# The second block of a weight sum: added by a transfer of POOL's queue, or by VectorE from a second tile

## The chip, the cores and the metric

The kernel runs on one core of a Trainium2 chip. The metric is the time of one execution in device microseconds (us). The core's engines run side by side, each in its own order: TensorE (PE, with PEld for its weight loads), VectorE (DVE), ScalarE (ACT), GpSimd (POOL) and SyncE (SP). SP, POOL and ACT also issue transfers (DMA); 16 DMA engines carry them out.

## The reference

A decoder layer in float32 on 512 tokens of width 2048. One input projection feeds two sorts of attention heads, eight MLA heads and eight forgetting-attention (FoX) heads; their gated outputs go through one output projection.

```python
h = _rms_norm(x, g_pre)
proj = h @ w_in                                   # 2048 x 6472
q_lat, kv_lat, k_rope_raw, gate_mla, fq, fk, fv, f_logit, gate_fox = split(proj)
o_mla = _mla_branch(q_lat, kv_lat, k_rope_raw, ..., w_uq, w_ukv, cos, sin) * silu(gate_mla)
o_fox = _fox_branch(fq, fk, fv, f_logit, b_forget) * silu(gate_fox)
o = concatenate([o_mla, o_fox], axis=-1) @ w_out  # 2048 x 2048
x = x + _rms_norm(o, g_post)
```

## The kernel before

**Matmuls.** Every float32 product is made of three passes: a weight is divided into a high part `whi` (ACT's copy) and a low part `wlo` (DVE's subtraction), the activations likewise, and `mm3` multiplies high by high, high by low and low by high.

**Chunks.** The weights are cut into 220 chunks, most of 128 x 1024 (512 KB), numbered in the order of their use. `load(i)` issues the transfer of chunk i into a raw place (`raw`), `divide(i)` makes `whi` and `wlo` of it, and the matmuls read these. `chunk(i)` is called when PE's code comes to chunk i: it loads up to `ahead_load` chunks ahead, divides up to `ahead` chunks ahead. A raw place is free again when its chunk has been divided. `raw_tile(i)` chooses the place: the pool `wp` (three), and beside it, by a rule on i, the pool `vr` in the first stage, `rw` (`deep`) in the middle stage, and `op` (`more`) in the last.

**Strassen-like products.** Four large projections, "v" (the FoX values), "l" (the latents), "m" (the MLA gate) and "o" (the output projection), use seven products of half-size blocks instead of eight: p1, p2, p4, q6, g5, g7, g3. Four of the seven multiply by a sum of weight blocks: p4 by t4, q6 by t6, g5 by t5, g7 by t7. t6 and t7 (for "o" also t4) are made in DRAM beside other work, in steps that `paced` counts off by `set_pace`: SP copies the first block, and a transfer of POOL's queue adds the second (`add_step`, line 320). The sums t4 and t5 of "v", "l" and "m" and t5 of "o" are used once, so they are not made in DRAM: the chunk is loaded from its first block and gets its second on the core. They are 32 chunks in eight fours:

- "v": 29 to 32 (g5) and 49 to 52 (p4)
- "l" and "m": 97 to 100 (p4 "l"), 105 to 108 (p4 "m"), 113 to 116 (g5 "m"), 121 to 124 (g5 "l")
- "o": 188 to 191 and 200 to 203 (the halves of g5)

For these, `load(i)` issues a second transfer on SP's queue into a tile `second`, and `join(i)` (line 269) adds it to the raw place on DVE, just before the division or one or two chunks ahead of it. `second` comes from `vr` (two) in "v", from `rw` (three, `EXTRA`) in "l" and "m", and otherwise from the general pool of 28 slots.

**Names in the rows.** PSUM banks name the products: `vg` is g5 and g3 of "v", `vp` p4 of "v", `gbl` p4 "l", `gbm` p4 "m", `gdl` g5 "l", `gdm` g5 and g3 of "m", `od` g5 and g3 of "o". `smg`, `sog` are activation sums divided for these products on the core; `awaymg`, `awayog` are such sums stored in DRAM by POOL and fetched again by SP (`bmg`, `bmq`, `bog`). `v_away` are stores of the FoX values, `ghf` and `gf` steps of the FoX gate, `lat` copies of the latents from PSUM. In rows of instructions the names carry their number.

**What sets the order.** The source order is spread over the engines by a scheduler that also places transfers; each engine then runs its row in order. A transfer on SP's or POOL's queue that must wait holds all that stand behind it in that row.

Of the kernel before, what the change touches and what calls it, by code (L numbers as in the profile page):

```python
# [12 lines left out]
F32 = mybir.dt.float32  # L13
# [3 lines left out]
ALU = mybir.AluOpType  # L17
AX = mybir.AxisListType

P = 128  # L20
# [24 lines left out]
KL = L4 + ROPE  # L45
HALF = S // 2
NSLOT = 28
DEEP, EXTRA = 6, 3


def split_const(c, bits, n):
# [15 lines left out]
def tile_hybrid_layer(  # L67
# [16 lines left out]
    nc = tc.nc  # L84
    pe, act, dve, pool = nc.tensor, nc.scalar, nc.vector, nc.gpsimd
# [10 lines left out]
    vr = v_room.enter_context(tc.tile_pool(name="vr", bufs=5))  # L96
# [3 lines left out]
    def slot(name, dt=F32, shape=(P, 2, S)):  # L100

        return sp.tile(list(shape), dt, tag="s", name=name)
# [105 lines left out]
    def add_chunks(w, cols, nk, per, width, first_k=0, single=0):  # L208


        first = len(chunks)
        k = 0
        while k < nk:
            n = min(1 if k < single else per, nk - k)
            chunks.append((w, cols, first_k + k, n, width))
            k += n
        return range(first, len(chunks))

    raws, ready, up_chunks, early = {}, {}, set(), set()

    more, deep, seconds = [], [], [vr, 2]
    needs = {}

    def raw_tile(i):
        if deep and deep[1] <= i < deep[2] and (i - deep[1]) % (DEEP + 3) < DEEP:
            return deep[0].tile([P, 1024], F32, tag="raw", name=f"raw{i}", bufs=DEEP)
        if i in up_chunks:
            return slot(f"raw{i}", shape=(P, 1024))
        if i <= prods["g7", "v"][-1] and i % 5 < 2:
            return vr.tile([P, 1024], F32, tag="raw", name=f"raw{i}", bufs=2)  # L230
        pool = more[0] if more and (i - more[1]) % 6 < 3 else wp
        return pool.tile([P, 1024], F32, tag="raw", name=f"raw{i}", bufs=3)

    def load(i, small=None):

        w, cols, k, n, width = chunks[i]
        assert state["step"] >= needs.get(i, -3) + 2
        if cols is None:

            raw = raw_tile(i)  # L240
            for a, b in alike(raw, w):
                nc.sync.dma_start(a, b)
            raws[i] = raw
            if k is not None:
                if seconds and i not in early:
                    pool, bufs = seconds
                    second = pool.tile([P, 2, 512], F32, tag="second", name=f"second{i}", bufs=bufs)
                else:
                    second = slot(f"second{i}")
                nc.sync.dma_start(second, k)  # L250
                raws[i] = raw, second.rearrange("p k c -> p (k c)")
            return
        if i < 2:
            raw = slot(f"raw{i}", shape=(P, 1024))
        else:
            raw = raw_tile(i)
        v = raw[:, : n * width].rearrange("p (k c) -> p k c", k=n)
        for at, off, cnt in cols:
            (nc.sync if cnt >= P or small is None else small).dma_start(
                v[:, :, at : at + cnt],  # L260
                w[0, k * P : (k + n) * P, off : off + cnt].rearrange("(k p) c -> p k c", p=P),
            )
        raws[i] = raw

    def join(i):

        if isinstance(raws.get(i), tuple):
            raw, second = raws[i]
            tc.keep_in_program_order(dve.tensor_tensor(out=raw, in0=raw, in1=second, op=ALU.add))  # L269
            raws[i] = raw  # L270

    def divide(i):
        w, cols, k, n, width = chunks[i]
        m = n * width
        join(i)
        raw = raws.pop(i)
        hi = wp.tile([P, 1024], F32R, tag="whi", name=f"whi{i}")
        lo = wp.tile([P, 1024], F32R, tag="wlo", name=f"wlo{i}")
        cast = act.copy(hi[:, :m], raw[:, :m])  # L279
        if deep:  # L280
            tc.keep_in_program_order(cast)
        dve.tensor_tensor(out=lo[:, :m], in0=raw[:, :m], in1=hi[:, :m].bitcast(F32), op=ALU.subtract)  # L282
        ready[i] = [t[:, :m].rearrange("p (k c) -> p k c", k=n) for t in (hi, lo)]

    state = {"loaded": 0, "divided": 0, "tiles": 0, "step": -1, "pace": 4}

    def prepare(i):
        while state["divided"] < min(len(chunks), i + 1):
            divide(state["divided"])
            state["divided"] += 1  # L290

    def chunk(i, ahead_load=4, ahead=2):
        upto = i + ahead_load
        if deep:
            upto = max(upto, min(i + DEEP + 2, deep[2] - 1, state["loaded"] + i % 2))
        while state["loaded"] < min(len(chunks), upto + 1):
            load(state["loaded"])
            state["loaded"] += 1
        prepare(i + ahead)
        for k in range(i + ahead + 1, min(state["loaded"], i + ahead + (3 if deep else 2))):  # L300
            join(k)
        return ready.pop(i)

    W, made = {}, {}
# [2 lines left out]
    def alike(to, w):  # L307

        if len(w.shape) == 4:
            to = to.rearrange("p (k h x) -> p k h x", k=2, h=4)  # L310
            return [(to[:, k], w[:, k]) for k in range(2)]
        return [(to if len(w.shape) == 2 else to.rearrange("p (k c) -> p k c", k=2), w)]
# [31 lines left out]
    prods = {}  # L344
# [45 lines left out]
    for n in ("g0", "p1", "g1", "p2", "g2", "s5", "q0", "s3", "k0", "s6", "p4", "s7",  # L390
              "q1", "k1", "q2", "k2", "q3", "k3", "g3"):
        name = {"p1": "p1", "p2": "p2", "p4": "p4", "s5": "g5", "s3": "g3", "s6": "q6", "s7": "g7"}.get(n)
        if name:
            add_products([(name, "v")], plain_in)
            if n == "s5":
                early.update(prods["g5", "v"][2:])
        else:
            at = {"q": O_FQ, "k": O_FK, "g": O_GF}[n[0]] + 256 * (3 - int(n[1]))
            fox[int(n[1])][n[0]] = add_chunks(w_in, [(0, at, 256)], NK, 4, 256)
# [9 lines left out]
    for n in ("q0", "p1", "k0", "q6", "p2", "p4", "g7", "q1", "g5", "k1", "g3", "q2", "k2", "q3", "k3"):  # L409
# [5 lines left out]
        p = int(n[1])  # L415
# [62 lines left out]

    load_x_tile(0)
    load(0, act)  # L480
    load_x_tile(1)
    load(1, act)
    load_x_part(1)
    load(2, act)
# [73 lines left out]
    def set_pace(n):  # L558
        state.update(pace=n, tiles=0)
# [685 lines left out]
    c22 = v_block("vc22")  # L1245
    scaled(c22, G, 2, pb, ALU.subtract, rcol)
    todo.extend([*f3, *rot[10:14], *d3, *rot[14:]])
    set_pace(8)
    q, wholes = fox_q(0)
    drain()  # L1250
    product("g3", "v", operand("g3", "m"), G, False, True)
# [3 lines left out]
    k = fox_k(0, wholes)  # L1255
# [17 lines left out]
    scaled(c21, C, 2, c21_sum, col=rneg)  # L1273
    v_out(c21, 1, 0)
    keys = [load_keys(6 + i, wholes) for i in range(2)]
    seconds.clear()
    v_room.close()
    pp = heads_room.enter_context(tc.tile_pool(name="pp", bufs=2, reuse_waits="tile"))
    set_pace(4.9)
# [3 lines left out]
    for p in range(4):  # L1283
        if p:
# [6 lines left out]
            k = fox_k(p, wholes)  # L1291
# [163 lines left out]
            state["loaded"], prods["g3", "m"][-1] + 1,  # L1455
        ]
    )
    seconds.extend([deep[0], EXTRA])
    for j in (1, 0):
        todo.append(  # L1460
            lambda j=j: todo.extendleft(
# [75 lines left out]
    for f in range(4, 8):  # L1537
        todo.append(lambda f=f: gate(f, c12, c22))
    deep.clear()
    seconds.clear()  # L1540
    room.close()
    pp = heads_room.enter_context(tc.tile_pool(name="pp", bufs=2, reuse_waits="tile"))
    qnh, qnl = zip(*(latents[i] for i in range(6)))
# [64 lines left out]
    for p in range(4):  # L1608
# [22 lines left out]
        k, kw = mla_k(p, wholes)  # L1631
# [157 lines left out]
    op = ctx.enter_context(tc.tile_pool(name="op", bufs=8, reuse_waits="tile"))  # L1789
# [10 lines left out]
    f = og_of[1, 0]  # L1800
# [30 lines left out]
    v = three(0, C, G, f)  # L1831
# [47 lines left out]
```

## Time and profile before

| what | value |
|---|---|
| runs shown (three) | 892.56, 892.96 and 895.5 us |
| median | 892.96 us |
| span of the profiled execution | 892.3 us |
| granted TensorE clock, mean | 0.998 |
| busy: PE / DVE / ACT / POOL | 880.3 / 660.2 / 462.1 / 72.8 us |
| DVE's joins (line 269) | 32, 39.0 us |
| transfers | 225.07 MB, mean 252 GB/s |

The span reaches from the first to the last instruction of the profiled execution; the page gives no other time of that execution. A group's row gives busy time, mean ns of one and the engine's idle time before it. In a row of a tile, three durations in ns (lowest, median, highest) are followed by the first and the last start in us. A row of a stretch gives busy time by engine, the granted clock, the mean busy share of the 16 DMA engines (it can read a little above 1) and the rate. The stages lie at about: "v" 64 to 230 us, FoX heads to 420, "l" and "m" 418 to 587, MLA heads to 713, "o" from there on.

### The profile page before, as it was taken

Reading aid. Unit: us, or ns where it says so; the run is one execution under the profiler, and the core shown is the slowest. Engines: PE = TensorE matmul, PEld = TensorE weight load, DVE = VectorE, ACT = ScalarE, POOL = GpSimd, SP = SyncE. Lnnn points to the kernel's source line nnn. Section 1 sums busy time; section 2 is a strip of 40 time slices with the busy share of each in tenths; the row PEclk is TensorE's granted clock in tenths of the full one; section 3 lists DMA queues with packets and bytes.
Section 4 is the critical chain, followed back from the end, with each engine's and each line's share of the span. In section 5 each row is a group of like instructions: output and inputs, shape, how many; then the busy total and the mean of one; then the engine's idle time right before and its main releaser. Section 6 shows DMA issues by size and latency. Waiting matters only on the chain.

```text
span 892.3 us, 12700 instructions
## 1 busy us (share of the span) xinstructions
PE 880.3 (99%) x4486; PEld 748.2 (84%) x4486; DVE 660.2 (74%) x1106; ACT 462.1 (52%) x841; POOL 72.8 (8%) x92
## 2 busy tenths in 40 slices
PE   9999999999999999999999999999999999999996
PEld 9988887888888888888998999788888888888885
DVE  4579995648665546477678999979787895988786
ACT  6944434334343433335455565657465776646383
POOL 0110110011110211010000000000000000000021
PEclk9999999999999999999999999999999999999999
DMA  9998798889999999997799885697988637799878
GB/s 319 277 265 241 212 341 279 250 214 315 261 282 275 238 230 225 247 231 186 243 412 410 329 303 178 167 275 166 221 182 215 153 111 233 228 323 322 264 214 254
DMA packets 139235, 225.07 MB, mean 252 GB/s; under 512 B 16898, under 2 KB 68892, under 8 KB 138148
## 3 DMA queue, kind: packets, MB, share of 16 engines
q1 hardware_dynamic: 124660, 184.19, 63.5%
q0 software_dynamic: 13776, 39.85, 22.2%
q8 instruction: 35, 0.57, 0.2%
q10 hardware_dynamic: 736, 0.22, 0.1%
q14 instruction: 28, 0.23, 0.1%
HBM read 209.53 MB, written 69.22 MB: 312 GB/s over the span
## 4 chain that ended last, share of the span: by engine, by line
PE 91%; DVE 4%; DMA 2%; ACT 2%; issue 1%; DVEq 0%; ACTq 0%; SPq 0%
PE fq L150 3%; PE fk L150 3%; PE fk L152 3%; PE fk L151 3%; PE fq L152 3%; PE fq L151 3%; PE fg L150 3%; PE in L614 3%; PE fg L151 3%; PE fg L152 3%; PE sm L657 3%; PE mq L152 2%; PE mq L150 2%; PE mq L151 2%; PE oa L150 2%; PE oa L152 2%
## 5 line engine op out<-in xcount | busy, mean ns | idle before, releaser
L282 DVE TENSOR_TENSOR wlo<-raw,whi 128x1024 fp32r<-128x1024 f32 (+3 forms) x220 | 261.0, 1189 | 134.0 <-ACT whi L279 125.8
L279 ACT CAST whi<-raw 128x1024 fp32r<-128x1024 f32 (+3 forms) x220 | 224.3, 1023 | 233.5 <-PE fk L151 31.8
L150 PE MATMUL fk<-h,whi 128*128 128x512 f32 x128 | 52.6, 411 | 0.0
L150 PE MATMUL fq<-h,whi 128*128 128x512 f32 x128 | 50.9, 397 | 0.0
L150 PE MATMUL fg<-h,whi 128*128 128x512 f32 x128 | 50.3, 393 | 0.0
L152 PE MATMUL fk<-h,wlo 128*128 128x512 f32 x128 | 50.2, 392 | 0.0
L151 PE MATMUL fk<-h,whi 128*128 128x512 f32 x128 | 50.2, 392 | 0.0
L152 PE MATMUL fq<-h,wlo 128*128 128x512 f32 x128 | 50.0, 391 | 0.0
L151 PE MATMUL fq<-h,whi 128*128 128x512 f32 x128 | 49.9, 390 | 0.0
L152 PE MATMUL fg<-h,wlo 128*128 128x512 f32 x128 | 49.9, 390 | 0.0
L151 PE MATMUL fg<-h,whi 128*128 128x512 f32 x128 | 49.9, 390 | 0.0
L675 ACT ACTIVATE pf<-pf,stf 128x128 f32<-128x128 f32 (+3 forms) x32 | 18.0, 562 | 61.4 <-DVE stf L666 61.4
L269 DVE TENSOR_TENSOR raw<-raw,second 128x1024 f32<-128x1024 f32 x32 | 39.0, 1219 | 0.5 <-DMA second<-in_w_out_dram 0.5
L614 PE MATMUL in<-whi,h 128*128 128x328 f32 x128 | 30.0, 321 | 0.0
L150 PE MATMUL mq<-ln,whi 128*128 128x512 f32 x72 | 29.2, 406 | 0.0
L152 PEld LDWEIGHTS fk<-h,wlo 128*128 128x128 f32 x128 | 24.1, 188 | 5.5
L152 PEld LDWEIGHTS fq<-h,wlo 128*128 128x128 f32 x128 | 24.0, 188 | 5.3
L152 PEld LDWEIGHTS fg<-h,wlo 128*128 128x128 f32 x128 | 24.0, 188 | 5.2
L151 PE MATMUL mq<-ln,whi 128*128 128x512 f32 x72 | 28.3, 393 | 0.0
L152 PE MATMUL mq<-ln,wlo 128*128 128x512 f32 x72 | 28.2, 392 | 0.0
L151 PEld LDWEIGHTS fg<-h,whi 128*128 128x128 f32 x128 | 24.1, 188 | 4.7
L150 PEld LDWEIGHTS fg<-h,whi 128*128 128x128 f32 x128 | 24.1, 188 | 4.7
(610 smaller groups left out, 2417.5 us busy)
## 6 DMA issues: line engine op xcount, KB each, us to landing
raw<-in_w_in_dram SPq DMA_DIRECT2D x96, 512.0 KB
raw<-in_w_out_dram SPq DMA_DIRECT2D x32, 512.0 KB
second<-in_w_in_dram SPq DMA_DIRECT2D x24, 512.0 KB
bmg<-awaymg SPq DMA_DIRECT2D x20, 256.0 KB
awaymg<-rmg POOLq DMA_DIRECT2D x8, 512.0 KB, 6.8
raw<-t6v SPq DMA_DIRECT2D x8, 512.0 KB
t7o<-in_w_out_dram SPq DMA_DIRECT2D x4, 1024.0 KB
t7o<-in_w_out_dram POOLq DMA_DIRECT2D x4, 1024.0 KB, 10.6
```

The source lines that it names most:

```text
L150: pe.matmul(o, ah, bh, start=first, stop=False, **kw)
L151: pe.matmul(o, ah, bl, start=False, stop=False, **kw)
L152: pe.matmul(o, al, bh, start=False, stop=last, **kw)
L269: tc.keep_in_program_order(dve.tensor_tensor(out=raw, in0=raw, in1=second, op=ALU.add))
L279: cast = act.copy(hi[:, :m], raw[:, :m])
L282: dve.tensor_tensor(out=lo[:, :m], in0=raw[:, :m], in1=hi[:, :m].bitcast(F32), op=ALU.subtract)
L614: pe.matmul(banks[t][:, :n], a[k][:, tss[t]], b[:, j, :], start=k == 0 and m == 0, stop=k == NK - 1 and m == 2,)
L657: pe.matmul(s[:, :nn], a[:, qs], c[:, :nn], start=(i == 0), stop=(i == len(pairs) - 1))
L675: act.activation(p, p, AF.Exp, bias=st[:, 0:1], scale=unit, accum_out=st[:, 1:2])
```

## The change

The second block goes straight into the raw place: `load` issues, on POOL's queue, a transfer that adds it there. `join`, the tiles `second` and what chose their place are gone. The room of the second tiles becomes raw places: `vr` has four instead of two (chunks by i % 7 < 4), `rw` nine instead of six (`DEEP`). `chunk` loads two further ahead in "v" and, through `DEEP`, eleven instead of eight in "l" and "m". One pace is 7 instead of 8.

```diff
-DEEP, EXTRA = 6, 3
+DEEP = 9
...
-        if i <= prods["g7", "v"][-1] and i % 5 < 2:
-            return vr.tile([P, 1024], F32, tag="raw", name=f"raw{i}", bufs=2)
+        if i <= prods["g7", "v"][-1] and i % 7 < 4:
+            return vr.tile([P, 1024], F32, tag="raw", name=f"raw{i}", bufs=4)
...
             raws[i] = raw
             if k is not None:
-                if seconds and i not in early:
-                    pool, bufs = seconds
-                    second = pool.tile([P, 2, 512], F32, tag="second", name=f"second{i}", bufs=bufs)
-                else:
-                    second = slot(f"second{i}")
-                nc.sync.dma_start(second, k)
-                raws[i] = raw, second.rearrange("p k c -> p (k c)")
+                pool.dma_start(raw.rearrange("p (k c) -> p k c", k=2), k, accum_op=ALU.add)
             return
...
-    def join(i):
-
-        if isinstance(raws.get(i), tuple):
-            raw, second = raws[i]
-            tc.keep_in_program_order(dve.tensor_tensor(out=raw, in0=raw, in1=second, op=ALU.add))
-            raws[i] = raw
-
     def divide(i):
         w, cols, k, n, width = chunks[i]
         m = n * width
-        join(i)
...
         upto = i + ahead_load
+        if i <= prods["g7", "v"][-1]:
+            upto = min(upto + 2, max(upto, prods["g7", "v"][-1]))
...
         prepare(i + ahead)
-        for k in range(i + ahead + 1, min(state["loaded"], i + ahead + (3 if deep else 2))):
-            join(k)
...
-    set_pace(8)
+    set_pace(7)
```

The order changes where chunks with a second block stand. Lines of the changed kernel are numbered 14 to 19 lower than in the old one.

**VectorE at g5 of "v", before** (`pos` and `nn` are steps of the rotary tables):

```order
L282 TENSOR_TENSOR wlo30_1381<-raw30_1288,whi30_1380 128x1024
L269 TENSOR_TENSOR raw31_1337<-raw31_1337,second31_1339 128x1024
L727 SCALAR_TENSOR_TENSOR ghf2_1423<-fg20_1248,rrow_214 128x512
L727 SCALAR_TENSOR_TENSOR ghf3_1427<-fg21_1249,rrow_214 128x512
L282 TENSOR_TENSOR wlo31_1436<-raw31_1337,whi31_1435 128x1024
L729 SCALAR_TENSOR_TENSOR gf2_1422<-gf2_1422,ghf2_1423 128x512
L729 SCALAR_TENSOR_TENSOR gf2_1422<-gf2_1422,ghf3_1427 128x512
L269 TENSOR_TENSOR raw32_1376<-raw32_1376,second32_1378 128x1024
L282 TENSOR_TENSOR wlo32_1455<-raw32_1376,whi32_1454 128x1024
```

The same place in the changed kernel:

```order
L268 TENSOR_TENSOR wlo30_1379<-raw30_1229,whi30_1378 128x1024
L711 SCALAR_TENSOR_TENSOR ghf2_1420<-fg20_1254,rrow_214 128x512
L711 SCALAR_TENSOR_TENSOR ghf3_1424<-fg21_1255,rrow_214 128x512
L268 TENSOR_TENSOR wlo31_1433<-raw31_1256,whi31_1432 128x1024
L713 SCALAR_TENSOR_TENSOR gf2_1419<-gf2_1419,ghf2_1420 128x512
L713 SCALAR_TENSOR_TENSOR gf2_1419<-gf2_1419,ghf3_1424 128x512
L268 TENSOR_TENSOR wlo32_1451<-raw32_1293,whi32_1450 128x1024
```

The joins are gone and the rest stands as it did.

**POOL at g5 of "v", before:**

```order
L953 DMA awaymg31_1152<-rmg31_1143 128x1024
L1194 DMA v_away0_226<-vc11_1243 128x2x256
L1194 DMA v_away1_227<-vc11_1243 128x2x256
L953 DMA awaymg52_1315<-rmg52_1303 128x1024
L953 DMA awaymg32_1332<-rmg32_1323 128x1024
L320 DMA t6v2_110<-t7v2_106 128x1024
```

and in the changed kernel:

```order
L937 DMA awaymg31_1156<-rmg31_1147 128x1024
L245 DMA raw29_1208<-in_w_in_dram 128x2x512
L245 DMA raw30_1229<-in_w_in_dram 128x2x512
L245 DMA raw31_1256<-in_w_in_dram 128x2x512
L245 DMA raw32_1293<-in_w_in_dram 128x2x512
L1178 DMA v_away0_226<-vc11_1249 128x2x256
L1178 DMA v_away1_227<-vc11_1249 128x2x256
L937 DMA awaymg52_1318<-rmg52_1306 128x1024
L937 DMA awaymg32_1335<-rmg32_1326 128x1024
```

Four accumulating transfers stand between the stores `awaymg31` and `v_away0`. In "l" and "m" the four of chunks 97 to 100 stand between the stores `awayog31` and `awayog50`, and the other twelve follow those, ahead of the background sums of "o".

**SP at the start of "l" and "m", before:**

```order
L242 DMA raw99_4209<-t6l2_126 128x1024
L259 DMA raw93_4107<-in_w_in_dram 128x2x512
L259 DMA raw94_4109<-in_w_in_dram 128x2x512
L259 DMA raw95_4129<-in_w_in_dram 128x2x512
L259 DMA raw96_4151<-in_w_in_dram 128x2x512
L242 DMA raw97_4153<-t6l0_124 128x1024
L250 DMA second97_4155<-in_w_in_dram 128x2x512
L242 DMA raw98_4178<-t6l1_125 128x1024
L250 DMA second98_4180<-in_w_in_dram 128x2x512
L250 DMA second99_4211<-in_w_in_dram 128x2x512
L242 DMA raw100_4213<-t6l3_127 128x1024
```

and in the changed kernel:

```order
L253 DMA raw102_4265<-in_w_in_dram 128x2x512
L253 DMA raw93_4091<-in_w_in_dram 128x2x512
L253 DMA raw94_4093<-in_w_in_dram 128x2x512
L253 DMA raw95_4113<-in_w_in_dram 128x2x512
L253 DMA raw96_4135<-in_w_in_dram 128x2x512
L242 DMA raw97_4137<-t6l0_124 128x1024
L242 DMA raw98_4161<-t6l1_125 128x1024
L242 DMA raw99_4191<-t6l2_126 128x1024
L242 DMA raw100_4194<-t6l3_127 128x1024
L971 DMA bmq60_4227<-awaymg50_1057 128x512
```

The second blocks are out of SP's row; chunk 97's first block stands in the same place, behind five loads of 512 KB, and those of 98 to 100 right behind it.

More of the change, by code (lines that the diff above doesn't have):

```diff
@@ L217, in add_chunks @@
         return range(first, len(chunks))
-    raws, ready, up_chunks, early = {}, {}, set(), set()
-    more, deep, seconds = [], [], [vr, 2]
+    raws, ready, up_chunks = {}, {}, set()
+    more, deep = [], []
     needs = {}
@@ L394, in tile_hybrid_layer @@
             add_products([(name, "v")], plain_in)
-            if n == "s5":
-                early.update(prods["g5", "v"][2:])
         else:
@@ L1275, in tile_hybrid_layer @@
     keys = [load_keys(6 + i, wholes) for i in range(2)]
-    seconds.clear()
     v_room.close()
@@ L1457, in tile_hybrid_layer @@
     )
-    seconds.extend([deep[0], EXTRA])
     for j in (1, 0):
@@ L1539, in tile_hybrid_layer @@
     deep.clear()
-    seconds.clear()
     room.close()
```

## The prediction

> **What bounds the kernel now.** I read the page first: the busy times and the chain that ended last.
>
> ```profile
> PE 880.3 (99%) x4486; PEld 748.2 (84%) x4486; DVE 660.2 (74%) x1106; ACT 462.1 (52%) x841; POOL 72.8 (8%) x92
> PE 91%; DVE 4%; DMA 2%; ACT 2%; issue 1%; DVEq 0%; ACTq 0%; SPq 0%
> ```
>
> TensorE (PE) is the bound: busy 880.3 of 892.3 us. A change elsewhere can only fill PE's holes or open new ones. Work taken from VectorE (DVE), busy 74%, is worth nothing where no matmul waits for it. So the next view is what PE itself waited for; the columns are us in total, times, longest.
>
> ```profile
> PE vg L150 <- ACT whi L279: 0.9, 1, 0.9
> PE gdm L151 <- DVE wlo L282: 0.8, 1, 0.8
> PE vg L151 <- DVE wlo L282: 0.8, 1, 0.8
> PE od L151 <- DVE wlo L282: 0.4, 1, 0.4
> ...
> 574.96 0.50 PE gdm L151
> ```
>
> The last row, from the chain in order of time, puts the wait on `gdm` at 575 us, in the last product of its stage, which adds no blocks. That leaves `vg` (product g5 of "v") and `od` (product g5 of "o"), where DVE joins two blocks per chunk. A lateness shorter than a matmul hides in busy time, so I compare how long equal products take, first to last start.
>
> ```profile
> L150 PE MATMUL vg<-whi,smg x16: 388/390/502, 130.1 to 142.5; 128*128 128x512 f32 x16
> L150 PE MATMUL vg<-whi,bmg x16: 389/389/390, 165.0 to 175.2; 128*128 128x512 f32 x16
> L150 PE MATMUL vp<-whi,h x16: 387/389/396, 208.5 to 219.1; 128*128 128x512 f32 x16
> L150 PE MATMUL gbm<-whi,h x16: 388/389/390, 480.6 to 490.8; 128*128 128x512 f32 x16
> ```
>
> The second is a product without a second block: 10.2 us. The first (g5 "v") takes 12.4, the third (p4 "v") 10.6, and the fourth (p4 "m", joined too) 10.2. So joining costs PE 2.2 + 0.4 us in "v" and nothing in p4 "m". In "o" the two halves of g5 show it in the same way, eight starts at a time:
>
> ```profile
> L150 PE MATMUL od<-whi,bog x8: 389/389/390, 795.0 to 799.7; 128*128 128x512 f32 x8
> L150 PE MATMUL od<-whi,sog x8: 388/389/390, 800.4 to 806.2; 128*128 128x512 f32 x8
> L150 PE MATMUL od<-whi,bog x8: 389/389/390, 828.6 to 833.4; 128*128 128x512 f32 x8
> L150 PE MATMUL od<-whi,sog x8: 388/389/398, 834.0 to 839.7; 128*128 128x512 f32 x8
> ```
>
> 5.8 against 4.7, and 5.7 against 4.8: another 2.0 us. All that this change could give back is therefore 2.2 + 0.4 + 2.0 = 4.6 us, half a per cent.
>
> **The change, part by part.** The joins go:
>
> ```profile
> L269 DVE TENSOR_TENSOR raw<-raw,second 128x1024 f32<-128x1024 f32 x32 | 39.0, 1219 | 0.5 <-DMA second<-in_w_out_dram 0.5
> ```
>
> 32 x 1.22 = 39.0 us leave DVE, worth the 4.6 us above if the sums are there in time. The 32 transfers of `second` leave SP's queue; 32 accumulating ones, of 524 kB each, enter POOL's. Each waits in POOL's row for its first block, holds everything behind it there, and costs POOL an issue. The nearest rows are POOL's accumulating transfers of blocks of the same size into DRAM, with their time to landing.
>
> ```profile
> t7v<-in_w_in_dram POOLq DMA_DIRECT2D x4, 512.0 KB, 8.3
> t7l<-in_w_in_dram POOLq DMA_DIRECT2D x4, 512.0 KB, 10.1
> t7m<-in_w_in_dram POOLq DMA_DIRECT2D x4, 512.0 KB, 10.6
> awaymg<-rmg POOLq DMA_DIRECT2D x8, 512.0 KB, 6.8
> ...
> DMA to landing us min/median/max: 6.9/9.4/11.3
> ```
>
> POOL is 8% busy, issues included, so the issues cost nothing. `awaymg` is a plain store. The last row is the only accumulation into SBUF, 256 KB each (line 1699, eight issued from 861.8 to 871.0). From 861.8 + 6.9 to about 871.0 + 11.3 eight of them land, 1.9 us apart, so I take 3.8 us between 524 kB ones in a row. How much engine time they take is in the stretches:
>
> ```profile
> core 0: us, PE busy (x) PEld busy (x) DVE busy (x) ACT busy (x) POOL busy (x), PEclk, DMA share, GB/s
> 447.00:459.00 12.00, 12.00 (x102) 12.00 (x102) 9.38 (x10) 6.92 (x10) 0.00 (x0) 1.00 1.04 408
> 867.00:872.00 5.00, 5.00 (x24) 4.14 (x23) 3.34 (x3) 3.90 (x6) 2.93 (x4) 1.00 1.10 188
> 480.00:500.00 20.00, 20.00 (x123) 18.02 (x122) 15.90 (x17) 10.71 (x13) 0.00 (x0) 1.00 0.89 331
> ```
>
> Plain loads fill the engines at 408 GB/s: 524 kB in 1.3 us. In the second stretch little but accumulation runs, and full engines move 188: 2.8 us. So a join's second block costs 1.5 us more DMA time than before, 48 us over 32 of them, and the place where that matters is the one where the engines are full already: 447 to 459 us.
>
> *g5 and p4 of "v".* In the old kernel the first blocks of g5 are issued here and copied here:
>
> ```profile
> 105.38 2.71 SPq L242 DMA_DIRECT2D raw<-in_w_in_dram  x2
> 114.27 0.37 SPq L242 DMA_DIRECT2D raw<-in_w_in_dram  x1
> 122.72 1.05 ACT L279 CAST whi<-raw 128x1024 fp32r<-128x1024 f32 x1
> ```
>
> Even issued no earlier, with 5 us for a load (four of 1.3 us in a row, an estimate) and 10.6 for the sum, the first is whole at 121 us, before its copy at 122.7. The last is whole at 130; without holes PE starts that chunk at 130.1 + 3 x 2.7 = 138.2 and needs it 2.3 us (copy and subtraction) earlier, at 136. Four places instead of two and two more chunks of lookahead bring the loads forward. DVE no longer has joins between the subtractions and `ghf` and `gf`. I book the whole 2.6 us. POOL now stores `v_away` and `awaymg` later, behind four sums; they are read tens of us later. The pace of 7 instead of 8 moves background sums ahead by some us. Both lie beside PE and are booked at nothing; if the later stores held up a place that ACT's row waits for, the hole would stay (a rival below).
>
> *p4 and g5 of "l" and "m": 16 chunks.* Here nothing is to be won and the sums come in fours. The first four (chunks 97 to 100):
>
> ```profile
> 435.63 2.73 SPq L259 DMA_DIRECT2D raw<-in_w_in_dram  x4
> 438.40 1.02 SPq L242 DMA_DIRECT2D raw<-t6l  x1
> 439.08 0.55 POOL L953 DMA_DIRECT2D awayog<-rog  x1 [1.41 <-DVE rog L963]
> 450.76 1.22 DVE L269 TENSOR_TENSOR raw<-raw,second 128x1024 f32<-128x1024 f32 x1
> ...
> L150 PE MATMUL gbl<-h,whi x32: 283/283/284, 458.2 to 469.4; 128*128 128x256 f32 x32
> ```
>
> Places open only at 435.6; chunk 97's first block is the fifth load, issued at 438.4 behind full engines. Its join at 450.8 bounds block and second, which stands 1.3 us behind, so the block is there at 448 to 449.5. Only then may POOL add: landing 8.3 to 10.6 us later, 456.6 to 459.5. PE starts the chunk at 458.2 and needs a copy (1.05) and a subtraction (1.22) first: the deadline is 455.8, and the sum is 0.8 to 3.7 late. I take 1.8, near the lower half, since POOL's row stands free from 439.6 on. The next three follow 3.8 us apart, while PE takes a chunk in (469.4 - 458.2) / 4, about 2.85 with the last start: 3 x 0.95 = 2.8 more. Behind the waiting copies in ACT's row stand the two copies of `lat` from PSUM and every later copy; behind POOL's sums stand the stores `awayog` and the background sums of "o", which nobody waits for before the "o" stage.
>
> While these four run, they take 11 us of full engines, which is eight plain loads. SP's row is in order, so chunks 101 to 108 and the `bmq` fetches come late by most of that; their lookahead of eleven chunks starts from nothing here. Chunks 105 to 108 then need four sums again, from 478 on. I take 1.4 for these (0 where the lookahead covers it, 4 where it doesn't), and nothing for the last eight, where the stretch of 480 to 500 shows engines free again (0.89) and 9 places lie ahead. Sum: 1.8 + 2.8 + 1.4 = 6.0 us lost, with ends of 2 and 12.
>
> The Trainium skill, page "DMA: Bandwidth & Descriptors", section on the anatomy of one transfer of the GpSimd path, fits 2.0 us plus the bytes at 436 GB/s: 3.2 us for one block, as an estimate. By it every sum would be in time and this term nothing. The trace has 8.3 to 10.6 for accumulating ones, and the measurement decides.
>
> *g5 of "o".* 2.0 us to win. The first blocks of the first half are issued here:
>
> ```profile
> 778.23 5.69 SPq L242 DMA_DIRECT2D raw<-in_w_out_dram  x3
> 787.45 0.41 SPq L242 DMA_DIRECT2D raw<-in_w_out_dram  x1
> ```
>
> Load (3.6, an estimate as above) and sum (10.6) make the first whole at 792.4; PE wants it 2.3 us ahead of 795.0, at 792.7. The next come 3.8 us apart at best, PE goes on by 2.7 a chunk: the fourth is some 3 late if it is added in a row, less by what PE loses there today (1.1). The second half starts with SP's row clear of second blocks, so I book it as won by most. Net gain 0.4 (bounds: all 2.0; or a loss of 2).
>
> **Sum.** Against the profiled span of 892.3: -2.6 + 6.0 - 0.4 = +3.0, 895.3. The page gives no other time of that execution; the runs shown are 892.56, 892.96 and 895.5, their median 0.7 above the span, so 896.0 us.
>
> **Rivals.** *The sums are hidden*: they land as POOL's plain stores do, some 7 us at most, or PE's slack covers them. Then the 4.6 us of holes close: 888.4. For it: p4 "m" runs its 10.2 us with joins in it, so there is slack; against it: the rows of 8.3 to 10.6. It decides if chunk 97's sum lands before 456. (The Trainium skill's fit, above, ends here too.)
> *The loads starve*: POOL's sums hold half the engines as long as they run, the plain loads of "l" and "m" fall behind in every group of four, not in the first alone. 16 sums x 1.5 us extra = 24 us of engine time, against 11% free engines, 2 us, from 480 to 500; a loss of about 12: 902. For it: the share of 1.04 from 447 to 459; against it: each us that PE is late gives the loads a us. It decides if chunk 108 is late by more than 4.
> *"v" keeps its hole*: ACT's copy of `smg`, right ahead of the first chunk's copy, waits for a store of `awaymg` today:
>
> ```profile
> 122.19 0.62 ACT L139 CAST smg<-rmg 128x512 fp32r<-128x512 f32 x1 [7.06 <-DMA awaymg<-rmg]
> ```
>
> POOL now issues that store behind four sums, 3.8 us each. If the place still hangs on it, the 2.6 us are not won: 898.6. Against it: two blocks that took places of the same pool are gone, and the new program names no transfer among what this copy waits for.
> *The sizes cancel*: the loss in "l" and "m" at its lower end, 2 to 4 us, against the 3 us won: no change. This is the lower half of the forecast's own range.
>
> **How the numbers follow.** A change under 0.3% (2.7 us) can't be told from none. Forecast, with its own range of 893.5 to 899: 0.54, of which 0.24 falls within 0.3%. Hidden: 0.20, all faster. Starved: 0.20, slower. "v" keeps its hole: 0.06, slower. That is faster 0.20, same 0.24, slower 0.56. The range takes the forecast, the starved case and the slower part of the hidden one: 889 to 904.
>
> **What would show it.** No join row on DVE; `vg<-whi,smg` in 10.2 us; new waits of ACT's copies (`whi`) for a transfer of POOL at 455 to 475 us, and a wait of PE on `gbl`, three or four times about a us; POOL's queue at 39.85 + 16.8 = 56.6 MB:
>
> ```profile
> q0 software_dynamic: 13776, 39.85, 22.2%
> ```
>
> Its share should rise by 32 x 2.8 / 892 = 10 points. Wrong if `gbl` starts at 456 or earlier without a hole (hidden), or if holes show at `gdm` and `gdl` as well (starved).

## The result, and the profile after

The changed kernel takes 917.94 us (median of 4 runs, 916.68 to 918.7) against 893.9 for the kernel before (4 runs): ratio 1.0269, 95% interval 1.0251 to 1.0287. The forecast was 896, with a range of 889 to 904. In all runs the time stands 1.8 us above the span (here 918.7 and 916.9), so the profiled execution of before, span 892.3, took 894.1.

The page of the profile after; busy times, then the chain that ended last, then POOL's queue:

```profile
PE 889.4 (97%) x4486; PEld 751.6 (82%) x4486; DVE 625.2 (68%) x1074; ACT 461.6 (50%) x841; POOL 112.1 (12%) x124
PE 75%; DMA 17%; DVE 4%; ACT 2%; issue 1%; SPq 0%; DVEq 0%; ACTq 0%; POOLq 0%
q0 software_dynamic: 22480, 56.63, 31.5%
```

PE is still busiest, but the chain now runs through transfers for 17% of the span instead of 2%: PE waits for DMA. POOL's queue moves the 56.6 MB that were foreseen and rose by 9.3 points. DVE lost its 32 joins. What PE waited for:

```profile
PE od L151 <- DVE wlo L268: 5.3, 7, 0.8
PE gbl L150 <- ACT whi L265: 2.4, 2, 2.1
...
PE gmt L1424 <- DVE gm L1426: 1.8, 1, 1.8
PE gdm L151 <- DVE wlo L268: 1.6, 2, 0.8
PE gdl L150 <- ACT whi L265: 1.5, 1, 1.5
PE gbm L151 <- DVE wlo L268: 1.4, 2, 0.8
```

Every product with sums behind "v" is in the list: `gbl`, `gbm`, `gdm`, `gdl`, and `od` seven times. The wait at `gmt` stands behind "l" and "m" (see the run on places). The equal products again, first to last start, eight starts at a time for `od`:

```profile
L150 PE MATMUL vg<-whi,smg x16: 389/389/390, 130.6 to 140.8; 128*128 128x512 f32 x16
L150 PE MATMUL gbl<-h,whi x32: 281/283/584, 458.3 to 474.5; 128*128 128x256 f32 x32
L150 PE MATMUL gbm<-whi,h x16: 386/389/497, 485.7 to 498.4; 128*128 128x512 f32 x16
L150 PE MATMUL od<-whi,bog x8: 388/390/505, 812.2 to 819.4; 128*128 128x512 f32 x8
L150 PE MATMUL od<-whi,sog x8: 387/394/503, 820.2 to 827.4; 128*128 128x512 f32 x8
```

`vg` takes its 10.2 us; `gbl` 16.2 instead of 11.2, `gbm` 12.7 instead of 10.2, and the two rows of `od`, which are the first half of g5 of "o", 7.2 each instead of 4.7 and 5.8. ACT's copies in "o", from the timeline (start, duration, in brackets the idle time before and what ended it), say when each sum was there:

```profile
811.12 1.04 ACT L265 CAST whi<-raw 128x1024 fp32r<-128x1024 f32 x1 [6.34 <-DMA raw<-in_w_out_dram]
815.07 1.05 ACT L265 CAST whi<-raw 128x1024 fp32r<-128x1024 f32 x1 [2.90 <-DMA raw<-in_w_out_dram]
819.13 1.05 ACT L265 CAST whi<-raw 128x1024 fp32r<-128x1024 f32 x1 [3.02 <-DMA raw<-in_w_out_dram]
...
823.11 1.05 ACT L265 CAST whi<-raw 128x1024 fp32r<-128x1024 f32 x1 [2.40 <-DMA raw<-in_w_out_dram]
```

Four sums, 4.0 us apart; PE takes a chunk in 2.75, so each after the first puts it some 1.2 us further behind. What the DMA engines do meanwhile (stretches; the last two columns are DMA share and GB/s):

```profile
core 0: us, PE busy (x) PEld busy (x) DVE busy (x) ACT busy (x) POOL busy (x), PEclk, DMA share, GB/s
811.00:819.00 8.00, 5.56 (x22) 3.67 (x21) 3.65 (x4) 2.09 (x2) 1.20 (x1) 1.00 1.10 262
844.00:846.00 2.00, 2.00 (x10) 1.66 (x9) 2.00 (x4) 1.10 (x4) 0.93 (x1) 1.00 1.07 193
```

Full engines move 262 GB/s while sums and plain loads share them, 193 where a sum runs almost alone. The packet records show why. Packets that started within 2 us, all 16 engines, median time of one:

| from, us | POOL's queue | SP's queue |
|---|---|---|
| 806 (after, "o") | 134 adding, 2 KB, 176 ns | 117 plain, 2 KB, 98 ns; 13 of 4 bytes |
| 850 (after, "o") | 131 adding, 2 KB, 176 ns; 11 of 4 bytes | 124 plain, 2 KB, 98 ns; 15 of 4 bytes |
| 478 (after, "m") | 97 adding, 2 KB, 176 ns; 15 of 4 bytes | 99 plain, 4 KB, 173 ns; 14 of 4 bytes |
| 822 (after, no sums) | 5 | 389 plain, 2 KB, 84 ns; 35 of 4 bytes |

An adding packet takes twice a plain one's time (at 4 KB 327 against 159 ns), and the engines take one packet from each queue in turn. The starts of the packets show the turns: from 848 to 855 us an adding packet is followed by the next adding one most often after 250 ns, and a plain one stands 150 ns behind it. Each engine has 16 adding packets of a block, and 16 x 250 ns are the 4.0 us between landings. Beside plain packets of 4 KB (476 to 481 us) the period is 320 to 330 ns, which makes 5.2 us for a block. The plain loads, which get one packet for each of POOL's, fall to some 120 GB/s where their packets have 2 KB, while PE consumes 524 kB in 2.75 to 2.85 us, 184 to 191 GB/s.

The Trainium skill bears on both: page "DMA: Bandwidth & Descriptors", section on queues, rings and completion order, says that each engine goes round its queues packet by packet. The records agree: with the packets of 4 bytes the counts are equal (134 to 130, 142 to 139, 112 to 113). The Trainium skill, page "Collectives: The Full Stack", part 3, says of the reduce step of a ring that "the add needs **two source reads**" and that it so runs at half a copy's rate; 176 against 84 ns agrees with that here.

Where the time went, by the first matmul of a chunk, against the same chunk of before (us; profiled executions differ by up to 1.2 us in places that no edit touched; the other kernels are those of the experiments):

| chunk (place) | after | "v" only | "v" and "o" | no add | last two | "v" and "o", 8 ahead |
|---|---|---|---|---|---|---|
| 29 (before g5 of "v") | +0.5 | +0.4 | +0.3 | +0.3 | -0.1 | -0.5 |
| 93 (before "l", "m") | -2.2 | -2.3 | -2.4 | -1.1 | -2.8 | -2.4 |
| 101 (after the 1st four) | +5.1 | -2.3 | -2.4 | -1.0 | +2.7 | -2.4 |
| 109 (2nd) | +7.6 | -2.3 | -2.4 | -1.0 | +2.7 | -2.4 |
| 117 (3rd) | +10.0 | -2.3 | -2.4 | -1.0 | +2.7 | -2.4 |
| 125 (4th) | +14.2 | -2.3 | -2.4 | -1.0 | +2.7 | -2.4 |
| 184 (before "o") | +16.2 | -2.3 | -0.4 | +1.0 | +7.0 | -2.5 |
| 192 (1st half of "o") | +21.3 | -2.1 | +6.2 | +1.4 | +11.2 | -1.9 |
| 208 (2nd half) | +24.7 | -2.1 | +10.6 | +1.0 | +10.8 | -0.5 |

So after: +0.5 at the start, -2.7 in "v", +16.4 in "l" and "m", +2.0 between them and "o", +8.5 in "o": +24.7.

One cost beside the waits runs through this table. After some pauses of PE the granted clock falls to 0.50 for 3.4 or 6.8 us, and PE then works at half its pace; the last section has the rows.

### The profile page after: what moved, and what is told of

It is laid out like the page before. It is cut to its first block, busy times and chain, and to the rows that moved or that the text cites. A ratio compares the mean times of both kernels' runs of the same rounds, so it can differ in the third digit from the quotient of the medians.

```text
span 916.9 us, 12690 instructions
## 1 busy us (share of the span) xinstructions
PE 889.4 (97%) x4486; PEld 751.6 (82%) x4486; DVE 625.2 (68%) x1074; ACT 461.6 (50%) x841; POOL 112.1 (12%) x124
## 4 chain that ended last, share of the span: by engine, by line
PE 75%; DMA 17%; DVE 4%; ACT 2%; issue 1%; SPq 0%; DVEq 0%; ACTq 0%; POOLq 0%
DMA raw<-in_w_out_dram 4%; DMA raw<-in_w_in_dram 4%; PE fq L150 3%; PE fk L150 3%; PE fk L152 3%; PE fk L151 3%; PE fq L152 3%; PE fq L151 3%; PE fg L150 3%; PE fg L152 3%; PE fg L151 3%; PE in L598 3%; PE sm L641 3%; DMA raw<-t6m 2%; DMA bmg<-awaymg 2%; DVE wlo L268 2%
## 5 line engine op out<-in xcount | busy, mean ns | idle before, releaser
L245 POOL DMA_DIRECT2D raw<-in_w_in_dram x24 | 29.4, 1257 | 84.9 <-DMA raw<-in_w_in_dram 26.0
## 6 DMA issues: line engine op xcount, KB each, us to landing
raw<-in_w_in_dram POOLq DMA_DIRECT2D x24, 512.0 KB, 12.4
```

The lines of the kernel that those rows point to most:

```text
L245: pool.dma_start(raw.rearrange("p (k c) -> p k c", k=2), k, accum_op=ALU.add)
```

## The experiments

Two theories. *Rate*: a sum holds the engines for 4.0 us where PE takes a chunk in 2.8, and a four falls behind by that. *Wait*: the second transfer cannot start before the first has landed, and comes late by itself. A third, *starved loads*, is the rival of the prediction: plain transfers get half the packets and come late. First, the change in "v" alone, in the kernel before, with its four places, its lookahead and its pace of 7:

```diff
-        if i <= prods["g7", "v"][-1] and i % 5 < 2:
+        if i <= prods["g7", "v"][-1] and i % 7 < 4:
...
-            if k is not None:
+            if k is not None and i <= prods["g7", "v"][-1]:
+                pool.dma_start(raw.rearrange("p (k c) -> p k c", k=2), k, accum_op=ALU.add)
+            elif k is not None:
...
```

> The kernel before, with the change made in "v" alone (four more places there, pace 7, second blocks added by POOL); "l", "m" and "o" are joined by DVE as before. The trace of the changed kernel shows PE 2.2 us ahead at the first g5 chunk behind "v", so what was forecast for "v" (2.6 us) should stand alone: 890.3, that is 2.6 under the kernel before (range 889.5 to 891.5). If the gain in "v" only shifted a wait to a later place of "l", where DVE joins again, the time stays at 893.

891.81 us, ratio 0.998 (0.9967 to 0.9994): about 2 us faster. That is 0.3 above the range, which was counted down from 892.96; the runs of the kernel before beside these have 893.99. The gain of "v" stands by itself, `vg` again takes 10.2 us:

```profile
L150 PE MATMUL vg<-whi,smg x16: 389/389/389, 130.5 to 140.7; 128*128 128x512 f32 x16
```

Is it the pace? The kernel before with `set_pace(7)` for `set_pace(8)`, nothing else:

> The kernel before with only the pace of the background sums of this stretch changed from 8 to 7. If the gain in "v" comes from the sums added by POOL (and the places and lookahead that go with them), nothing moves: 893.9, ratio 1.000. If the earlier background sums carried it, 892 as with the whole change in "v".

893.51 us, ratio 0.9998 (0.9988 to 1.0008): nothing. Its profile shows 0.6 us won at chunk 33, too little to tell. Whether the four places and the longer lookahead would win the same with DVE still adding was not run, so what POOL's addition itself gives in "v" is not shown.

Then "o" as well, with "l" and "m" still joined by DVE:

```diff
-            if k is not None and i <= prods["g7", "v"][-1]:
+            if k is not None and not deep:
```

> "v" and "o" added by POOL, "l" and "m" joined by DVE. If the losses are local to each group of four, "o" costs what the offsets of the changed kernel's PE show, 5.1 + 3.4 = 8.5 us: 890.3 + 8.5 = 898.8 (897 to 900.5), and the remaining 19 of the changed kernel belong to "l" and "m". If "o" is late because the earlier stages left its loads or background sums late, it is hidden here and the time stays under 893.

902.8 us (899.43 to 904.52), ratio 1.0094 (1.0075 to 1.0112). By the medians it stands 11 us behind "v" alone, more than the 8.5 expected (898.8 was a miss); by the same account 15.1 of the changed kernel's loss belong to the edits in "l" and "m". The profiled execution took 904.52: 11.0 us go in "o" and 1.9 before it, with a wait of 1.1 us at a copy `mw` in the attention. In "o" chunk 191's first block was asked for at 784.8, and POOL issued its sum only at 797.5, 12.7 us later, with three sums running beside; behind these waits the clock was at 0.50 from 810.3 to 813.6, which the changed kernel's "o" does not have.

What the addition itself costs: the changed kernel, without it.

```diff
-                pool.dma_start(raw.rearrange("p (k c) -> p k c", k=2), k, accum_op=ALU.add)
+                pool.dma_start(raw.rearrange("p (k c) -> p k c", k=2), k)
```

> The changed kernel, POOL's transfer overwrites the place and does not add: the sum is left out, but issue, place, queue and the wait for the first block are the same. Theory rate: a packet of 2 KB that adds takes 176 ns on its engine and alternates with a plain one of 98, so sums land 4.0 us apart and PE takes a chunk in 2.8; without the addition a packet takes 84, 16 x (84 + 98) = 2.9 us between landings, and nearly all holes inside the fours go: 898 (895 to 903). Theory wait: what costs is that the second transfer may start only when the first has landed, whatever it does then: the holes stay, 912 to 918.

895.09 us, ratio 1.0003 (0.9991 to 1.0014). The order, the places and the wait for the first block are the same, and 22.8 of the 24 us are gone. ACT's copies of the first four, and a stretch of "m":

```profile
454.57 1.05 ACT L265 CAST whi<-raw 128x1024 fp32r<-128x1024 f32 x1 [4.96 <-DMA raw<-in_w_in_dram]
457.83 1.05 ACT L265 CAST whi<-raw 128x1024 fp32r<-128x1024 f32 x1 [2.21 <-DMA raw<-in_w_in_dram]
...
459.74 1.06 ACT L265 CAST whi<-raw 128x1024 fp32r<-128x1024 f32 x1
...
470.00:480.00 10.00, 10.00 (x46) 8.28 (x45) 6.17 (x7) 5.40 (x8) 1.42 (x2) 1.00 1.03 417
```

The same transfers land in 4.7 to 10.4 us, median 7.3, instead of 6.7 to 18.8, median 12.4, and full engines move 417 GB/s. One thing besides the addition has changed: POOL's packets of these blocks now have 4 KB (from 454 us 133 of them in 2 us, 159 ns each, against 134 plain ones of 2 KB), so a block needs 8 turns instead of 16, and most of the transfers land 1.8 to 2.5 us apart where 2.9 was expected. In the next run the adding packets of the p4 fours have 4 KB as well, and its time hardly moves; so it is above all the adding that costs, by its engine time. It does not follow that the wait is free: it is shorter here too. The clock stays at 1.00 up to the last 7 us of this profile, so what the clock cost behind late sums is gone with them.

Do the engines take turns by packet? In p4 the operands are exchanged, so that the adding packets have 4 KB and the plain ones 2. The edit reaches p4 of "v" too, which the expectation does not count:

```diff
-                    W[name, g][j] = (W["t6", g][j], b21) if name == "t4" else (first, second)
+                    W[name, g][j] = (b21, W["t6", g][j]) if name == "t4" else (first, second)
```

> The changed kernel, with the two operands exchanged in p4 of "l" and "m": the weight block (rows of 2 KB) is loaded first, the finished sum t6 (rows of 4 KB) is added. An adding packet of 4 KB takes 328 ns, so the engine time of a block is the same (8 x 328 against 16 x 176). If the engines alternate packet by packet between the two queues, a block now lets 8 plain packets through instead of 16: 8 x (328 + 98) = 3.4 us between landings instead of 4.0 in chunks 97 to 100 and 105 to 108, and 3 to 4 us are won in all: 914 (912.5 to 916). If the two queues share by bytes or time, nothing moves: 918.

917.29 us, ratio 1.0263 (1.0249 to 1.0276): no gain, so the price was a miss. The mechanism shows all the same:

```profile
458.24 1.04 ACT L266 CAST whi<-raw 128x1024 fp32r<-128x1024 f32 x1 [8.02 <-DMA raw<-t6l]
461.49 1.04 ACT L266 CAST whi<-raw 128x1024 fp32r<-128x1024 f32 x1 [2.21 <-DMA raw<-t6l]
...
464.58 1.05 ACT L266 CAST whi<-raw 128x1024 fp32r<-128x1024 f32 x1 [1.08 <-DVE wlo L269]
468.11 2.00 ACT L266 CAST whi<-raw 128x1024 fp32r<-128x1024 f32 x2 [2.48 <-DMA raw<-t6l]
```

The sums land 3.2 to 3.4 us apart instead of 3.9 to 4.7, with 79 packets of 4 KB against 78 of 2 KB in 2 us; an adding packet follows the last most often after 400 ns, and 8 x 400 are 3.2 us. The first four lose 5.2 us instead of 7.3. But the sums began 2 us later, and the four of g5 "m" lose 5.5 instead of 2.4: at chunk 125 it stood at +13.1 against +14.2, of which nothing reached the end. That faster sums starve the loads more would fit, but is not shown: the clock stood at 0.50 from 522.5 to 525.8 (g5 "m") and from 822.8 to 829.6 ("o"), where the changed kernel's did not.

Fewer sums: of each four outside "v" the first two are joined by DVE, the last two (`by_pool`) added by POOL. Against the kernel with "v" alone:

```diff
-DEEP, EXTRA = 6, 3
+DEEP, EXTRA = 7, 2
...
-            if k is not None and i <= prods["g7", "v"][-1]:
+            if k is not None and (i <= prods["g7", "v"][-1] or i in by_pool):
```

> "v" added by POOL; of each four in "l", "m" and "o" the first two are joined by DVE and the last two added by POOL. Theory rate: two sums take 8 us while PE takes 11 for the four, and PE reaches the third chunk 5.6 us after the first, so the engines keep pace and most of the 25 us go: 892 plus at most 1 us per four, 892 to 898. Theory wait: each sum is late by itself, since it can start only after its first block has landed and takes 9 to 13 us: half of the loss stays, 892 + 12 = 904 (901 to 907).

904.94 us, ratio 1.0125 (1.0103 to 1.0147). The number is that of the theory of the wait, but its places are not: of four groups in "l" and "m" three lose nothing (table), where rate says so, and half a loss in each was expected from wait. The first loses 5.5 us, before and in chunk 99. POOL's timeline:

```profile
434.68 1.24 POOL L246 DMA_DIRECT2D raw<-in_w_in_dram  x1 [26.89 <-DMA raw<-t6l]
...
453.85 1.22 POOL L246 DMA_DIRECT2D raw<-in_w_in_dram  x1 [16.10 <-DMA raw<-t6l]
```

Its first block was asked for at 437.2 and landed at 453.8, behind full engines (share 1.05 from 440 to 454); the sum landed 9 us later, at 463.0. That is the wait. The same took 4.2 us in the first half of "o", and 4.3 went at `gmt`, the place of the next run. Behind each of the three the clock was at 0.50 for 3.4 us (from 465.7, 813.9 and 598.8), up to 1.7 us each by half the pace, so that the time came out at 904 is in part luck. Both theories hold, at different places: the wait sets the first sum of a group that starts from nothing; that rate and starved loads make the rest is read from the other runs.

The 2.0 us before "o" stand in the kernel that does not add as well, so they are not the sums. The first `w_uq` blocks (chunks 141 to 143) are asked for 7 us before their copy; the changed order of places leaves them behind chunks 138 to 140. Those three get places of the nine:

```diff
-        if deep and deep[1] <= i < deep[2] and (i - deep[1]) % (DEEP + 3) < DEEP:
+        if deep and deep[1] <= i < deep[2] and ((i - deep[1]) % (DEEP + 3) < DEEP or i >= deep[2] - 3):
```

> The changed kernel; the last three chunks of the "l" and "m" stage (138 to 140) are given places of the nine instead of the three of the general pool, so the first w_uq blocks (chunks 141 to 143) need not wait for their division. The changed kernel asks for them at 590 us, 7 us before their copy; the one with "v" alone 19 us before. If the 2.0 us hole at the gate's transposes (gmt) comes from that order of places, it goes: 915.9 (915 to 917). If it comes from the late sums, it stays: 918.

915.85 us, ratio 1.0243 (1.0215 to 1.0271). SP's rows, after and in this kernel:

```profile
590.24 8.32 SPq L253 DMA_DIRECT2D raw<-in_w_uq_dram  x12
```

```profile
555.79 3.98 SPq L253 DMA_DIRECT2D raw<-in_w_uq_dram  x6
```

The wait at `gmt` is gone from its list, and chunks 137 and 184 stand equally late (+13.7 both). By the times 2 us were won; the intervals overlap, so the profile carries this verdict.

Can the sums of "o" be hidden by asking earlier? The changed kernel, with slots for the eight blocks and asked for eight chunks ahead (`soon` holds the two fours of g5 of "o"):

```diff
+        if i + 8 in soon:
+            load(i + 8)
         while state["loaded"] < min(len(chunks), upto + 1):
-            load(state["loaded"])
+            if state["loaded"] not in raws:
+                load(state["loaded"])
```

> The changed kernel; the first and the second blocks of the two fours of "o" (chunks 188 to 191 and 200 to 203) are asked for eight chunks ahead of PE instead of four, into slots of their own. Theory rate: four sums need 4 x 4.0 = 16 us behind the first block's landing whatever the order, so what hides them is to begin about 16 + 5 us before PE wants the first; asked for some 12 us earlier, all four are there in time, "o" loses none of its 8.5 us and the 2.0 us of its old joins go too: 907.4 (906 to 910). Theory starved loads: the plain loads of the chunks in between get every second packet only and come late instead, and the holes move there: 913 to 918.

911.8 us, ratio 1.0194 (1.0175 to 1.0213): 6.1 of the 8.5 us are back, the 2.0 are not. It lies between the two ranges and decides for neither. The same edit on the kernel with "v" and "o":

> "v" and "o" added by POOL, with the blocks of "o" asked for eight chunks ahead; "l" and "m" joined by DVE as before. Theory rate: 1.9 us won in "v" (as the kernel with "v" alone) and 2.0 in "o": 889.5 to 890 against 893.9, ratio 0.9955. Theory starved loads: "o" gives back what it wins and more: 892 to 902.

893.55 us, ratio 0.9993 (0.998 to 1.0005), in the range of the starved loads. It is 9 us better than without it, but the gain of "v" is used up: chunk 191's sum landed at 799.9, too late by a little (0.6 us lost in that half), and chunk 199's plain load, put behind the first blocks of the second half, was copied only at 823.2 and cost 1.5 us. Rate and starved loads, one each. Asked for nine ahead:

> As the kernel that adds "v" and "o" on POOL and asks eight chunks ahead in "o", but nine ahead. There chunk 191's sum was 1.2 us late and the plain load of chunk 199, put behind the four of the second half, 1.5 us. Nine ahead puts the first blocks some 5 us earlier, the fourth sum at 795 where 798 is wanted, and chunk 199's load before the last of the four only by one. Theory rate: the sums are all in time, what is lost in "o" is at most the 1.5 of chunk 199, and the 2.0 of the old joins are won: 889.5 to 891.5. Theory starved loads: another plain load comes late instead: 893 or more.

890.75 us, ratio 0.9967 (0.9951 to 0.9983), as rate says. Against "v" alone (0.998) the intervals overlap, so for the gain in "o" the profile has to speak. The `od` rows, two for each half:

```profile
L150 PE MATMUL od<-whi,bog x8: 389/389/389, 796.3 to 801.1; 128*128 128x512 f32 x8
L150 PE MATMUL od<-whi,sog x8: 389/389/389, 801.7 to 806.5; 128*128 128x512 f32 x8
L150 PE MATMUL od<-whi,bog x8: 389/389/389, 828.9 to 833.7; 128*128 128x512 f32 x8
L150 PE MATMUL od<-whi,sog x8: 389/389/389, 834.4 to 839.1; 128*128 128x512 f32 x8
```

4.8, 4.8, 4.8 and 4.7 us, no hole in them. From chunk 184 to 208 it gains 1.4 us on the kernel before. (This profiled execution took 893.9; it has a wait of 1.1 us, a copy `mw` in the attention, that "v" alone has not, and behind it the clock at 0.50 from 611.6 to 614.9.) Does it need POOL? "v" alone on POOL, "o" joined by DVE with both blocks asked for eight ahead, and each join one chunk earlier in DVE's row:

```diff
-        for k in range(i + ahead + 1, min(state["loaded"], i + ahead + (3 if deep else 2))):
+        for k in range(i + ahead + 1, min(state["loaded"], i + ahead + (3 if deep or more else 2))):
```

> "v" alone is added by POOL; "o" is joined by DVE, with both blocks of its fours asked for eight chunks ahead and each join placed one chunk earlier in DVE's row, ahead of the subtraction of the chunk before. Plain loads cost half the engine time of adding ones, and DVE needs 2 x 1.22 = 2.5 us for a chunk of PE's 2.75. If the 2.0 us that "o" lost before came from the row join, copy, subtraction, 3.6 us in a chain for each chunk, it goes: 889.5 to 890.5, ratio 0.9955. If the blocks' landing limited it, nothing moves against "v" alone: 892.

890.87 us, ratio 0.9969 (0.9956 to 0.9982): the same. This run changes two things, when the blocks are asked for and where the joins stand, and so can't tell the two readings of its expectation apart. The kernel before can. Its DVE, in the first half of g5 of "o":

```profile
795.92 1.23 DVE L282 TENSOR_TENSOR wlo<-raw,whi 128x1024 fp32r<-128x1024 f32 x1
797.06 1.22 DVE L269 TENSOR_TENSOR raw<-raw,second 128x1024 f32<-128x1024 f32 x1
799.53 1.23 DVE L282 TENSOR_TENSOR wlo<-raw,whi 128x1024 fp32r<-128x1024 f32 x1 [1.25 <-ACT whi L279]
800.68 1.22 DVE L269 TENSOR_TENSOR raw<-raw,second 128x1024 f32<-128x1024 f32 x1
```

The join starts as soon as the subtraction of the chunk before is done, without a wait for a transfer; then DVE waits for ACT's copy of the joined chunk. From one subtraction to the next that makes 3.6 us, against 2.75 that PE takes. So the 2.0 us of "o" were the row of join, copy and subtraction behind one another, not the joins' time on DVE; POOL's sums or an earlier place in the row take it away.

## Why the prediction was wrong

- *"v"*: right. -2.6 forecast, -2.7 in the profile, `vg` in 10.2 us; the rival "keeps its hole" did not come.
- *The first four of "l"*: the mechanism was right, the size was not: 1.8 + 2.8 forecast, 7.3 lost. The first sum was foreseen for 456.6 to 459.5 (the terms given there, 448 to 449.5 and 8.3 to 10.6, add up to 456.3 to 460.1); its copy starts at 457.2 and PE loses 2.3. The next three cost 3.9, since the sums come 3.9 to 4.7 us apart and not 3.8. The low part of the last chunk, which had no term, costs 1.1. PE pauses 2.1 us at `gbl`, and the granted clock is 0.63 from 456 to 464 (row at the end), so chunk 97 itself takes 6.1 us; that is made up by chunk 100, which waits for its sum in any case.
- *The later fours*: the step that failed. "1.4 for these", "nothing for the last eight", since the share of 0.89 in the kernel before showed free engines and nine places lie ahead. They lost 2.5, 2.4 and 4.2. A share measured without sums says nothing of a stretch that has them: from 482 to 490 it is now 1.09, at 274 GB/s. The lookahead did what was hoped for: in each of the three fours the first chunk was divided 2.4 to 3.4 us before PE came to it. But behind it the sums landed 3.8 to 5.5 us apart and PE takes a chunk in 2.7 to 2.9, the same difference that was counted for the first four, so the lead was gone by the third or fourth chunk. ACT's copies in p4 "m":

```profile
481.06 1.05 ACT L265 CAST whi<-raw 128x1024 fp32r<-128x1024 f32 x1 [1.71 <-DMA raw<-in_w_in_dram]
...
486.33 1.05 ACT L265 CAST whi<-raw 128x1024 fp32r<-128x1024 f32 x1 [3.69 <-DMA raw<-in_w_in_dram]
...
490.04 1.05 ACT L265 CAST whi<-raw 128x1024 fp32r<-128x1024 f32 x1 [0.98 <-DVE bmq L140]
494.12 1.99 ACT L265 CAST whi<-raw 128x1024 fp32r<-128x1024 f32 x2 [3.02 <-DMA raw<-in_w_in_dram]
```

- All four start less than 0.2 us after their sum landed (480.9, 486.2, 490.0 and 494.0).
- The rival "the loads starve" named the sign (holes at `gdm` and `gdl`) and a loss of 12 us, which is 16.4; but only part of that is plain loads. By what stood last before ACT's copies, about 11 of the 16.4 us lie behind sums (the first two fours and more than half of the third) and about 5 behind plain fetches of `bmg` (the rest of the third, and the last with what the clock took there).
- The 4.2 of the last four are that rival. The sum of chunk 124 was there by 540.2; ACT stood before it, for plain fetches, and PE paused 1.5 and 0.8 us. Some 1.7 more went to the clock behind these pauses (rows at the end), for which the prediction has no term anywhere:

```profile
542.23 0.62 ACT L139 CAST bmg<-bmg 128x512 fp32r<-128x512 f32 x1 [4.90 <-DMA bmg<-awaymg]
...
544.09 0.62 ACT L139 CAST bmg<-bmg 128x512 fp32r<-128x512 f32 x1 [0.70 <-DMA bmg<-awaymg]
544.61 1.04 ACT L265 CAST whi<-raw 128x1024 fp32r<-128x1024 f32 x1
```

- *"o"*: the second step that failed: -0.4 forecast, +8.5 came. The first sum was booked for 792.4, from a load of 3.6 us; the block took 5.4 from its issue to POOL's (794.4 to 799.8), and the sum 11.2 (to 811.0). The working itself had "the next come 3.8 us apart", then booked the second half "as won by most". Four sums in a row, 4.0 us apart against PE's 2.75 a chunk, lose 3.7 us even when the first is just in time, and this holds in each half. With the 3.8 taken it is some 3, which the prediction wrote down for the first half and not for the second.
- *The order of places*: +2.0 before "o" was not in the sum at all. The places of "l" and "m" were counted, not followed to the stage behind.
- *The Trainium skill's fit* for one transfer (page "DMA: Bandwidth & Descriptors"; 3.2 us) would have made every sum timely; adding transfers took 6.7 to 18.8, and the measurement decided rightly.
- *From span to time*: 1.8 us, not 0.7.

What stays open: how much of the lateness of the sums comes from their own pace, and how much from first blocks that the starved queue brought late. Of the experiments none takes away one and leaves the other; the one without addition takes both.

## What to carry to other kernels

An accumulating transfer is paid in DMA engine time, about twice a plain one's, and the other queue pays as well, since the engines take turns by packet: count the period of one packet of each queue (here 250 ns) times the packets of a block on one engine (16). Before a join is moved from an engine with room to a DMA queue, compare time per block when both queues are busy (here 4.0 us) with the consumer's time per block (2.8): where it is longer, each further block of a run adds the difference to its lateness, unless the run starts that much earlier. A lead for the first block is not enough, as the later fours show. The change paid only where blocks were asked for long before they were needed ("v", and by the profile "o" at nine chunks ahead), and in "o" joining earlier in DVE's row won the same.

## What the runs showed of the hardware

An adding packet into SBUF takes 176 ns for 2 KB and 327 for 4 KB, plain ones 84 and 159. POOL's issue of an adding transfer takes 1.21 us, of a plain one 0.72. A pause of PE can be dearer than its length. From the changed kernel at `gbl`, then at `gdl`, and from the kernel with "v" and "o" in "o":

```profile
456.00:464.00 8.00, 5.41 (x25) 4.95 (x24) 3.05 (x3) 3.06 (x4) 0.57 (x1) 0.63 1.10 260
545.00:550.00 5.00, 3.54 (x16) 3.34 (x17) 4.29 (x6) 5.00 (x9) 0.00 (x0) 0.69 1.01 410
806.00:812.00 6.00, 4.20 (x14) 2.85 (x13) 4.16 (x5) 3.47 (x4) 0.00 (x0) 0.85 0.75 253
```

After the pause of 2.1 us the matmuls of `gbl` start 0.21 us apart until 465, instead of 0.12. The clock is at 0.50 for 6.8 us there, for 3.4 us after pauses of 1.5 and 0.8 us at `gdl`, and for 3.4 us after pauses of 0.8, 1.0 and 0.8 us within 6 us in "o" of the third row. Pauses of about a us in "o" of the changed kernel left it at 1.00, so the length of one pause does not decide it; what does is not shown. The Trainium skill, page "TensorE: Matmul & The Clock Gate", part 1, tells of a half-rate state after an idle window of some 3.4 us; here pauses shorter than that were followed by it.
